# Block products of the delta-rule inverse with B and K together as stationary, in a two-layer RWKV-7 / RG-LRU / mLSTM kernel

## The chip, the cores and the metric

One core of one Trainium2 chip runs the program. The metric is the device time of one execution in microseconds, the median of several runs. TensorE (PE) does matmuls, VectorE (DVE) and ScalarE (ACT) the elementwise work, GpSimd (POOL) little, and SyncE (SP) issues the transfers.

## The reference

The input x is 256 tokens of 2048 features, in float32. Layer 0 (an RG-LRU head group beside an mLSTM head group) is not touched by the change. Layer 1 is RWKV-7 time mixing with 64 heads of 64 features:

```python
u = h @ w_in                                  # columns r, k, v, z, 4096 each
rkv = rkv + (shift_right(rkv) - rkv) * mu_rkv
...                                           # decay w, gate a, kk normalised per head
def step(S, inp):
    r_t, w_t, k_t, v_t, kk_t, a_t = inp
    sa = jnp.einsum('bhvk,bhk->bhv', S, -kk_t)
    S = (S * w_t[:, :, None, :] + sa[..., None] * (kk_t * a_t)[:, :, None, :]
         + v_t[..., None] * k_t[:, :, None, :])
    return S, jnp.einsum('bhvk,bhk->bhv', S, r_t)
...
y = head_norm(y, ...) + bonus                 # bonus = sum(r * k * r_k) * v, per head
return (y * jax.nn.silu(z)) @ w_out
```

The kernel does the scan in four chunks of 64 tokens. In a chunk each token has four rows of 64 features: A (from kk and the decay), R (from r), B (from kk and a) and K (from k). The products of B and K with A and R, masked to earlier tokens, give the matrices of the chunk. The one of B with A has to be inverted (as one minus a strictly triangular matrix).

## The kernel before

Layer 1 works through eight groups g of four feature tiles (128 features, two heads each). Per group there are four in_proj's, in the order k, r, z, v. Each is 192 matmuls into a `gb` bank, from a moving operand of 256 tokens, in pieces of weights split in a high and a low part (`whi`, cast by ACT, and `wlo`, subtracted by DVE, from `raw`). There are three buffers of each, so that wlo of a piece waits until PE is through with the piece three before. After the last group comes out_proj, whose moving operands are split the same way (`yh`, `yl`).

Everything else is written as generators that a class `Weave` (line 58) runs between the matmuls of the stream: four lanes, each generator in a lane after the one before, and each `yield x` says how many microseconds, by the plan, to let pass before its next piece. Lane 0 has `blocks` (927) and `inverse` (986), lane 1 `scores` (951), `values` (1048), `recur` (1089) and `final`, lane 2 `norm`, and lane 3 `decay` and `keys`. The main loop also drains some of them at fixed places: the scores after the z projection, the values of the group before after k. The order in which pieces come out of this is the program's order: PE runs strictly in it (`InOrder`, 102), and so do DVE and ACT as queues. A wait of one instruction therefore holds all that stands behind it on its engine.

The steps of a group that the change touches, in the order of their data:

- `keys` writes AR columns 0:64 (A), Gn (a norm per head) and BK, with B and K next to each other: for one head's 64 rows, B in its own half of the 128 columns and K in the other half.
- `blocks` multiplies, for tile f, chunk c and head hd, 64 columns of BK (B alone, the stationary operand) with A's 64 columns of AR. There are 32 such products, 64x64 each, in two banks (`mbank`; there are four of them); DVE multiplies them with Gn into Aab.
- `scores` writes R into AR's columns 64:128 (four DVE instructions `AR<-rt,Pe`), then takes for each tile f eight products of the whole BK (128 columns) with the whole AR (A and R), 128x128 each, in two banks, and four transposes of BK into a third (L120, then ACT's copy to BKt). DVE masks the banks into At, with `rmask`, in two instructions of 128x512 per tile.
- `inverse` transposes Aab (Ab), solves by 31 pairs of DVE instructions `tf`, `Tb`, waits for recur of the group before, transposes the result into TT and ZT, and finishes it with two sets of small products on PE (`mb<-ZT,Aab`, then with TT).
- `values` makes the bonus: bi, bh and bl from R and K, UV by products with `centre`, the sums by `bonesr`, and vt times them.
- `recur` runs the four chunks with At, BKt, UV and TT.

At, BKt, TT and Rc have one buffer each. L117 and L120 are the lines of the helper through which all matmuls and transposes pass, and L133 that of the elementwise instructions; so the trace tells them apart by their tiles. `f2` counts pairs of tiles.

Of the kernel before, what the change touches and what calls it, by code (L numbers as in the profile page):

```python
# [11 lines left out]
ADD, SUB, MUL, MAX, MIN = ALU.add, ALU.subtract, ALU.mult, ALU.max, ALU.min  # L12

P = 128
# [130 lines left out]
def two_layers(ctx, tc, x, gpost, cst, selc, v0, v1, w_in0, w_out0, w_in1, w_out1, lruw, qkvw,  # L145
               wif, gbias, lora1, lora2, out):
    nc = tc.nc
    act, dve, pool, pe = nc.scalar, nc.vector, nc.gpsimd, nc.tensor
    PS = bass.MemoryType.PSUM
    wv_ = Weave(tc, 4)  # L150
    pe = wv_.pe = InOrder(tc, pe)
    dve, act = Behind(tc, dve), Behind(tc, act)
# [13 lines left out]
    def mbank():  # L166
        return pm.tile([P, 512], F32, name="mb", tag="mb")

    cs = base.tile([P, NC1], F32, name="cs")
    ident = cs[:, C_ID:C_ID + 128]  # L170
# [249 lines left out]
    with ExitStack() as l0:  # L420
# [180 lines left out]
        gt = c0.tile([8, 7, T], F32, name="gt", tag="wg")  # L601
# [119 lines left out]
        for c in range(4):  # L721
# [6 lines left out]
            for f in range(4):  # L728
                i = 4 * c + f
# [44 lines left out]
    with ExitStack() as l1:  # L774
        c1 = l1.enter_context(tc.tile_pool(name="c1", bufs=1))
        g1 = l1.enter_context(tc.tile_pool(name="g1", bufs=1))
        rmask = cs[:, C_RM:C_RM + 128]
# [9 lines left out]
        def gt(name, tag, shape=(4, T), dt=F32, bufs=1):  # L787
            return g1.tile([P, *shape], dt, name=name, tag=tag, bufs=bufs)
# [98 lines left out]
        def keys(g, st):  # L887
# [36 lines left out]
                    yield 0.6  # L924
            st.update(Gn=Gn, AR=AR, BK=BK)

        def blocks(g, st):

            yield from until(st["keys"])
            AR, BK, Gn = st["AR"], st["BK"], st["Gn"]  # L930
            yield 3.5
            Aab = g1.tile([P, 4, 2, 4, 64], F32, name="Aab", tag="c8")
            bs = [mbank(), mbank()]
            for f2 in range(2):
                for f in range(2):
                    for c in range(4):
                        for hd in range(2):
                            hr = slice(64 * hd, 64 * hd + 64)
                            n = (f * 4 + c) * 64
                            pe.matmul(bs[f2][hr, n:n + 64], lhsT=BK[hr, 2 * f2 + f, c, 64 * hd:64 * hd + 64], rhs=AR[hr, 2 * f2 + f, c, 0:64],  # L940
                                      start=(n == 0), stop=True, skip_group_check=True)
            yield 0.5
            for f2 in range(2):
                for hd in range(2):
                    hr = slice(64 * hd, 64 * hd + 64)
                    dve.tensor_tensor(Aab[0:64, 2 * f2:2 * f2 + 2, hd, :, :], bs[f2][hr].rearrange("p (f c i) -> p f c i", f=2, c=4),
                                      Gn[hr, 2 * f2:2 * f2 + 2, :].unsqueeze(3).broadcast_to([64, 2, 4, 64]), MUL)
                    yield 0.9
            st["Aab"] = Aab

        def scores(g, st):
            rt, AR, BK, Pe = st["r"], st["AR"], st["BK"], st["Pe"]
            yield 0.36
            for f in range(4):
                dve.tensor_tensor(AR[:, f, :, 64:128], c4(rt[:, f, :]), Pe[:, 4 * f:4 * f + 4, 1:65], MUL)
                yield 0.5
            yield 2
            Rc = gt("Rc", "Rc", (4, 4, 64))
            act.copy(Rc, AR[:, :, :, 64:128])

            At = gt("At", "At", (4, 2, 4, 128))
            BKt = gt("BKt", "BKt", (4, 4, 128))
            rm4 = rmask.unsqueeze(1).broadcast_to([P, 4, 128])
            for f in range(4):
                ab = [mbank(), mbank()]
                for c in range(4):
                    for hd in range(2):
                        hr = slice(64 * hd, 64 * hd + 64)
                        pe.matmul(ab[hd][:, 128 * c:128 * c + 128], lhsT=BK[hr, f, c, :], rhs=AR[hr, f, c, :],
                                  start=(c == 0), stop=True, skip_group_check=True)  # L970
                b = mbank()
                for c in range(4):
                    pe.transpose(out=b[:, c * P:(c + 1) * P], in_=BK[:, f, c, :], identity=ident)
                yield 0.42
                for hd in range(2):
                    v = ab[hd].rearrange("p (c j) -> p c j", c=4)
                    dve.tensor_tensor(At[:, f, hd, :, :], v, rm4, MUL)
                    yield 1.12
                act.copy(BKt[:, f, :, :], b.rearrange("p (c j) -> p c j", c=4))
            for hd in range(2):  # L980
                hr = slice(64 * hd, 64 * hd + 64)
                act.copy(At[hr, :, hd, :, 0:64], AR[hr, :, :, 0:64])
                yield 0.3
            st.update(At=At, BKt=BKt, Rc=Rc)

        def inverse(g, st):
            Aab = st["Aab"]
# [101 lines left out]
        def recur(g, st):  # L1089
            yield from until(st["inv"])  # L1090
            At, BKt, UV, Rc, Gn, PC, TTv = (st[n] for n in ("At", "BKt", "UV", "Rc", "Gn", "PC", "T"))
# [5 lines left out]
            for c in range(4):  # L1097
                wb = mbank()
                for f in range(4):
                    for hd in range(2):  # L1100
                        hr = slice(64 * hd, 64 * hd + 64)
                        kr = slice(0, P) if c else slice(64 * (1 - hd), 64 * (1 - hd) + 64)
                        pe.matmul(wb[hr, f * 64:(f + 1) * 64], lhsT=At[kr, f, hd, c, 0:64], rhs=UV[kr, c, f, hd, :],
                                  start=(f == 0), stop=True, skip_group_check=True)
# [51 lines left out]
                    yield 0.25  # L1156
                if c == 1:
                    nm = wv_.add(norm(0, Yb, Yn, Yn[:, 1]), 2)
            yT = gt("yT", "Rc", (2, 4, P))
            yield from until(nm)  # L1160
            yield from norm(1, Yb, Yn, yT[:, 1].rearrange("p f (h v) -> p f h v", h=2))
# [186 lines left out]
```

## Time and profile before

| | |
|---|---|
| median of 3 runs | 1887.37 us (1884.68 to 1888.13) |
| the profiled execution | 1884.82 us, span 1883.0 us |
| granted TensorE clock, mean | 0.996 of full |
| PE busy | 1856.2 us, 99% |
| PE's weight loads (PEld) busy | 1723.5 us, 92% |
| DVE busy | 1400.9 us, 74% |
| ACT busy | 1052.2 us, 56% |
| DMA, mean | 161 GB/s |

A fp32 matmul of the program is two instructions in the trace. A row of a timeline gives the start, how long, the engine, the line, what is written from what (out<-in), for PE the rows and columns of the weights and then those of the output, how many instructions follow each other, and in brackets the idle time before the row and who ended it. Ends of PE's instructions are modelled, and its rows overlap; start to start is the safer measure.

### The profile page before, as it was taken

The page shows a single profiled execution, that of the slowest core. Times are in us where ns is not written, and L with a number is a line of the kernel's source. Part 1 is how long each engine was busy: PE and PEld are TensorE (multiplying, and loading weights), DVE is VectorE, ACT ScalarE, POOL GpSimd, SP SyncE. Part 2 cuts the span into 40 slices and gives each one's busy share as a digit, 9 for nine tenths or more (in the row PEclk, how much of TensorE's full clock was granted, in tenths as well). Part 3 has the DMA queues.
Part 4 walks back from the last instruction along what each step waited for, and adds up shares of the span by engine and source line. Part 5 has one row for each costly group of instructions (what it writes and reads, how often), then busy time and mean ns, then how long its engine had stood idle before and what let it go on. Part 6 is the DMA issues. An engine that isn't in the chain of part 4 may idle for free.

```text
span 1883.0 us, 39445 instructions
## 1 busy us (share of the span) xinstructions
PE 1856.2 (99%) x16410; PEld 1723.5 (92%) x16411; DVE 1400.9 (74%) x2279; ACT 1052.2 (56%) x1626; POOL 63.4 (3%) x94
## 2 busy tenths in 40 slices
PE   9999999999999999999999999999999999999998
PEld 8999999999888898999999999999999999987886
DVE  6777777767455668888689789698797896895554
ACT  5446566645444455565565656656656656565442
POOL 0000000000000100000010000000100100000000
PEclk9999999999999999999999999999999999999999
DMA  7543554446566353433433334344344343355654
GB/s 254 189 156 135 180 179 168 158 169 227 194 208 210 138 170 133 147 122 124 147 132 136 136 132 158 124 144 149 119 152 141 131 146 128 130 193 202 214 204 151
DMA packets 95314, 302.66 MB, mean 161 GB/s; under 512 B 11160, under 2 KB 20120, under 8 KB 95136
## 3 DMA queue, kind: packets, MB, share of 16 engines
q1 hardware_dynamic: 95136, 300.16, 46.5%
q8 instruction: 128, 2.10, 0.5%
q14 instruction: 50, 0.41, 0.1%
HBM read 292.25 MB, written 7.86 MB: 159 GB/s over the span
## 4 chain that ended last, share of the span: by engine, by line
PE 92%; DVE 5%; issue 1%; ACT 1%; DMA 1%; POOL 0%; SPq 0%; DVEq 0%; POOLq 0%; ACTq 0%
PE gb L117 75%; PE mb L117 15%; DVE wlo L133 2%; PE mb L120 2%; DVE Tb L133 0%; DVE tf L133 0%; DMA raw<-in_w_in_dram 0%; DVE yT L133 0%; DVE rt L133 0%; ACT whi L133 0%; DMA xq<-in_x_dram 0%; DVE hl L133 0%; POOL vr L1186 0%; DVE AR L133 0%; DVE Ab L133 0%
## 5 line engine op out<-in xcount | busy, mean ns | idle before, releaser
L133 DVE TENSOR_TENSOR wlo<-raw,whi 128x1024 fp32r<-128x1024 f32 (+1 forms) x517 | 627.2, 1214 | 316.7 <-ACT whi L133 278.6
L133 ACT CAST whi<-raw 128x1024 fp32r<-128x1024 f32 (+1 forms) x517 | 538.5, 1044 | 519.5 <-PE gb L117 454.6
L117 PE MATMUL gb<-hh,whi 128*128 128x256 f32 x3120 | 791.6, 290 | 0.6 <-ACT whi L133 0.6
L117 PE MATMUL gb<-hl,whi 128*128 128x256 f32 x3120 | 771.9, 283 | 0.5 <-DVE hl L133 0.5
L117 PEld LDWEIGHTS gb<-hh,whi 128*128 128x128 f32 x3120 | 597.9, 192 | 8.8 <-ACT whi L133 0.8
L117 PEld LDWEIGHTS gb<-hl,whi 128*128 128x128 f32 x3120 | 598.7, 192 | 2.0 <-DVE hl L133 1.1
L117 PE MATMUL gb<-hh,wlo 128*128 128x256 f32 x3120 | 454.5, 286 | 0.0
L117 PEld LDWEIGHTS gb<-hh,wlo 128*128 128x128 f32 x3120 | 405.2, 191 | 3.8
L117 PE MATMUL gb<-whi,yl 128*128 128x512 f32 x500 | 137.2, 392 | 2.0 <-DVE yl L133 2.0
L117 PE MATMUL gb<-whi,yh 128*128 128x512 f32 x500 | 136.2, 391 | 0.0
L117 PE MATMUL gb<-wlo,yh 128*128 128x512 f32 x500 | 135.9, 391 | 0.0
L117 PEld LDWEIGHTS gb<-whi,yl 128*128 128x128 f32 x500 | 93.0, 188 | 22.2 <-DVE yl L133 2.9
L117 PEld LDWEIGHTS gb<-wlo,yh 128*128 128x128 f32 x500 | 93.4, 188 | 19.7
L117 PEld LDWEIGHTS gb<-whi,yh 128*128 128x128 f32 x500 | 93.1, 188 | 19.4
L133 DVE TENSOR_TENSOR Tb<-Tb,tf 64x31 f32<-64x31 f32 (+15 forms) x248 | 82.6, 333 | 6.2
L133 DVE TENSOR_TENSOR tf<-Ab,Tb 64x31 f32<-64x31 f32 (+15 forms) x248 | 81.9, 330 | 4.5
L117 PE MATMUL mb<-AR,BK 64*128 64x128 f32 (+1 forms) x1024 | 60.8, 258 | 11.6 <-DVE AR L133 6.0
L117 PEld LDWEIGHTS mb<-AR,BK 64*128 64x128 f32 (+1 forms) x1024 | 52.3, 165 | 18.5 <-PE gb L117 7.0
L133 DVE TENSOR_TENSOR UV<-mb,Gn 64x256 f32<-64x256 f32 x64 | 27.0, 422 | 34.8 <-PE mb L117 33.6
L117 PEld LDWEIGHTS mb<-UV,At 128*64 128x64 f32 (+1 forms) x1024 | 35.0, 137 | 10.3 <-issue 2.5
L117 PE MATMUL mb<-UV,At 128*64 128x64 f32 (+1 forms) x1024 | 43.8, 228 | 0.0
L133 ACT ACTIVATE zz<-kP,dv 128x256 f32<-128x256 f32 x64 | 32.3, 505 | 20.5 <-DVE BK L133 10.7
(264 smaller groups left out, 1773.1 us busy)
## 6 DMA issues: line engine op xcount, KB each, us to landing
raw<-in_w_in_dram SPq DMA_DIRECT2D x384, 512.0 KB, 3.3
raw<-in_w_out_dram SPq DMA_DIRECT2D x128, 512.0 KB, 4.3
wr<-in_wif_dram SPq DMA_DIRECT2D x48, 80.0 KB, 2.4
y1d<-zt SPq DMA_DIRECT2D x7, 512.0 KB, 3.4
yraw<-y1d SPq DMA_DIRECT2D x7, 512.0 KB, 3.7
xq<-in_x_dram SPq DMA_DIRECT2D x8, 256.0 KB, 5.6
lw<-in_lruw_dram SPq DMA_DIRECT2D x4, 512.0 KB, 4.6
xr<-in_x_dram SPq DMA_DIRECT2D x8, 256.0 KB, 5.7
```

Source lines behind the costliest of these rows:

```text
L117: return self._chain(self.eng.matmul(*a, **k))
L120: return self._chain(self.eng.transpose(**k))
L133: r = op(*a, **k)
```

## The change

Inverse's products in `blocks` take the 128 columns of BK as the stationary operand instead of B's 64, with the same moving columns of A. So a product gives B's rows (for Aab) and K's rows (At's columns of A) at once, in two banks per pair of tiles, one for each head. `blocks` now also masks K's rows into At (four instructions of 64x512) and makes four transposes of BK in each of its halves: `turned` does those of one tile and ACT's copy to BKt (tiles 0 and 1 in `blocks`, 2 and 3 in `scores`). Since At and BKt have one buffer each, `blocks` starts only when `recur` of the group before has set "used". `scores` is left with the moving columns 64:128 (R) and does two tiles at a time; it waits until the blocks have At, and its pause ahead of the products is 6.2 where it was 2.

```diff
@@ -924,29 +924,46 @@
                     yield 0.6
             st.update(Gn=Gn, AR=AR, BK=BK)
 
+        def turned(BKt, BK, f):
+            b = mbank()
+            for c in range(4):
+                pe.transpose(out=b[:, c * P:(c + 1) * P], in_=BK[:, f, c, :], identity=ident)
+            act.copy(BKt[:, f, :, :], b.rearrange("p (c j) -> p c j", c=4))
+
         def blocks(g, st):
 
             yield from until(st["keys"])
             AR, BK, Gn = st["AR"], st["BK"], st["Gn"]
             yield 3.5
+            while g and "used" not in sts[g - 1]:
+                yield 0.44
             Aab = g1.tile([P, 4, 2, 4, 64], F32, name="Aab", tag="c8")
-            bs = [mbank(), mbank()]
+
+            At = gt("At", "At", (4, 2, 4, 128))
+            BKt = gt("BKt", "BKt", (4, 4, 128))
             for f2 in range(2):
+                fs = slice(2 * f2, 2 * f2 + 2)
+                bs = [mbank(), mbank()]
                 for f in range(2):
                     for c in range(4):
                         for hd in range(2):
                             hr = slice(64 * hd, 64 * hd + 64)
                             n = (f * 4 + c) * 64
-                            pe.matmul(bs[f2][hr, n:n + 64], lhsT=BK[hr, 2 * f2 + f, c, 64 * hd:64 * hd + 64], rhs=AR[hr, 2 * f2 + f, c, 0:64],
+                            pe.matmul(bs[hd][:, n:n + 64], lhsT=BK[hr, 2 * f2 + f, c, :], rhs=AR[hr, 2 * f2 + f, c, 0:64],
                                       start=(n == 0), stop=True, skip_group_check=True)
-            yield 0.5
-            for f2 in range(2):
+                turned(BKt, BK, f2)
+                yield 0.5
                 for hd in range(2):
                     hr = slice(64 * hd, 64 * hd + 64)
-                    dve.tensor_tensor(Aab[0:64, 2 * f2:2 * f2 + 2, hd, :, :], bs[f2][hr].rearrange("p (f c i) -> p f c i", f=2, c=4),
-                                      Gn[hr, 2 * f2:2 * f2 + 2, :].unsqueeze(3).broadcast_to([64, 2, 4, 64]), MUL)
+                    dve.tensor_tensor(Aab[0:64, fs, hd, :, :], bs[hd][hr].rearrange("p (f c i) -> p f c i", f=2, c=4),
+                                      Gn[hr, fs, :].unsqueeze(3).broadcast_to([64, 2, 4, 64]), MUL)
                     yield 0.9
-            st["Aab"] = Aab
+                for hd in range(2):
+                    kr = slice(64 * (1 - hd), 64 * (1 - hd) + 64)
+                    dve.tensor_tensor(At[kr, fs, hd, :, 0:64], bs[hd][kr].rearrange("p (f c i) -> p f c i", f=2, c=4),
+                                      rmask[kr, 0:64].unsqueeze(1).unsqueeze(1).broadcast_to([64, 2, 4, 64]), MUL)
+                    yield 0.9
+            st.update(Aab=Aab, At=At, BKt=BKt)
 
         def scores(g, st):
             rt, AR, BK, Pe = st["r"], st["AR"], st["BK"], st["Pe"]
@@ -954,34 +971,32 @@
             for f in range(4):
                 dve.tensor_tensor(AR[:, f, :, 64:128], c4(rt[:, f, :]), Pe[:, 4 * f:4 * f + 4, 1:65], MUL)
                 yield 0.5
-            yield 2
+            while "At" not in st:
+                yield 0.44
+            yield 6.2
             Rc = gt("Rc", "Rc", (4, 4, 64))
             act.copy(Rc, AR[:, :, :, 64:128])
-
-            At = gt("At", "At", (4, 2, 4, 128))
-            BKt = gt("BKt", "BKt", (4, 4, 128))
-            rm4 = rmask.unsqueeze(1).broadcast_to([P, 4, 128])
-            for f in range(4):
+            At, BKt = st["At"], st["BKt"]
+            for f2 in range(2):
                 ab = [mbank(), mbank()]
-                for c in range(4):
-                    for hd in range(2):
-                        hr = slice(64 * hd, 64 * hd + 64)
-                        pe.matmul(ab[hd][:, 128 * c:128 * c + 128], lhsT=BK[hr, f, c, :], rhs=AR[hr, f, c, :],
-                                  start=(c == 0), stop=True, skip_group_check=True)
-                b = mbank()
-                for c in range(4):
-                    pe.transpose(out=b[:, c * P:(c + 1) * P], in_=BK[:, f, c, :], identity=ident)
+                for f in range(2):
+                    for c in range(4):
+                        for hd in range(2):
+                            hr = slice(64 * hd, 64 * hd + 64)
+                            n = (f * 4 + c) * 64
+                            pe.matmul(ab[hd][:, n:n + 64], lhsT=BK[hr, 2 * f2 + f, c, :], rhs=AR[hr, 2 * f2 + f, c, 64:128],
+                                      start=(n == 0), stop=True, skip_group_check=True)
+                turned(BKt, BK, 2 + f2)
                 yield 0.42
                 for hd in range(2):
-                    v = ab[hd].rearrange("p (c j) -> p c j", c=4)
-                    dve.tensor_tensor(At[:, f, hd, :, :], v, rm4, MUL)
+                    dve.tensor_tensor(At[:, 2 * f2:2 * f2 + 2, hd, :, 64:128], ab[hd].rearrange("p (f c i) -> p f c i", f=2, c=4),
+                                      rmask[:, 64:128].unsqueeze(1).unsqueeze(1).broadcast_to([P, 2, 4, 64]), MUL)
                     yield 1.12
-                act.copy(BKt[:, f, :, :], b.rearrange("p (c j) -> p c j", c=4))
             for hd in range(2):
                 hr = slice(64 * hd, 64 * hd + 64)
                 act.copy(At[hr, :, hd, :, 0:64], AR[hr, :, :, 0:64])
                 yield 0.3
-            st.update(At=At, BKt=BKt, Rc=Rc)
+            st.update(Rc=Rc)
 
         def inverse(g, st):
             Aab = st["Aab"]
@@ -1156,6 +1171,7 @@
                     yield 0.25
                 if c == 1:
                     nm = wv_.add(norm(0, Yb, Yn, Yn[:, 1]), 2)
+            st["used"] = True
             yT = gt("yT", "Rc", (2, 4, P))
             yield from until(nm)
             yield from norm(1, Yb, Yn, yT[:, 1].rearrange("p f (h v) -> p f h v", h=2))
```

Where the pieces then stand follows from the weave. Three places are shown, in the program's order (a name is out<-in, then the shape of the output and how often the row repeats).

TensorE in the first group, at the first block products. Before, all 32 in a row and then the first scores:

```order
L117 MATMUL gb<-hh,whi 128x256
L117 MATMUL gb<-hl,whi 128x256
L117 MATMUL mb<-AR,BK 64x64 x32
L117 MATMUL gb<-hh,whi 128x256
L117 MATMUL gb<-hl,whi 128x256
L117 MATMUL gb<-hh,whi 128x256
L117 MATMUL gb<-hl,whi 128x256
L117 MATMUL mb<-AR,BK 128x128 x8
L120 MATMUL mb<-cs,BK 128x128 x4
L117 MATMUL gb<-hh,wlo 128x256 x8
```

Now 16 of them, with four transposes (`mb<-cs,BK`), and the stream goes on:

```order
L117 MATMUL mb<-AR,BK 128x64 x16
L120 MATMUL mb<-cs,BK 128x128 x4
L117 MATMUL gb<-hh,whi 128x256
L117 MATMUL gb<-hl,whi 128x256
L117 MATMUL gb<-hh,whi 128x256
L117 MATMUL gb<-hl,whi 128x256
L117 MATMUL gb<-hh,wlo 128x256 x8
```

The other 16 stand 40 stream matmuls behind these, and the scores, which stood four behind, 136.

TensorE at the blocks of a later group. Before, they stood in the middle of the last chunk of recur (`mb<-UV,At`, `mb<-Sn,Rc`):

```order
L117 MATMUL mb<-UV,At 64x64 x8
L117 MATMUL gb<-hh,whi 128x256
L117 MATMUL gb<-hl,whi 128x256
L117 MATMUL gb<-hh,whi 128x256
L117 MATMUL gb<-hl,whi 128x256
L117 MATMUL mb<-Sn,Rc 64x64 x8
L117 MATMUL gb<-hh,whi 128x256
L117 MATMUL gb<-hl,whi 128x256
L117 MATMUL gb<-hh,whi 128x256
L117 MATMUL gb<-hl,whi 128x256
L117 MATMUL mb<-AR,BK 64x64 x32
```

Now the same neighbours, with half the blocks and transposes:

```order
L117 MATMUL mb<-Sn,Rc 64x64 x8
L117 MATMUL gb<-hh,whi 128x256
L117 MATMUL gb<-hl,whi 128x256
L117 MATMUL gb<-hh,whi 128x256
L117 MATMUL gb<-hl,whi 128x256
L117 MATMUL mb<-AR,BK 128x64 x16
L120 MATMUL mb<-cs,BK 128x128 x4
```

Both follow recur's last products closely; but in the stream of in_proj the blocks and recur with them now stand 92 matmuls later (the second half of the blocks 128), and the first scores 116.

VectorE at the end of the inverse of a later group (the transposes TT and ZT). Before, the values (bi, vt, bl) follow them:

```order
L133 TENSOR_TENSOR Tb<-Tb,tf 64x31
L133 TENSOR_TENSOR wlo<-raw,whi 128x1024
L133 STREAM_TRANSPOSE TT<-Tb 32x32x32 x2
L133 TENSOR_TENSOR wlo<-raw,whi 128x1024
L133 STREAM_TRANSPOSE ZT<-Tb 32x32x32
L133 TENSOR_TENSOR wlo<-raw,whi 128x1024
L133 TENSOR_TENSOR bi<-Rc,BK 64x1024 x2
```

Now they stand ahead of them, bi, vt and bl among the pairs tf, Tb, and vt by mb between TT and ZT:

```order
L133 SCALAR_TENSOR_TENSOR vt<-gb,vec_81,vt 128x255 x2
L133 TENSOR_TENSOR tf<-Ab,Tb 64x135
L133 SCALAR_TENSOR_TENSOR bl<-bi,vec_81,bh 128x256
L133 TENSOR_TENSOR wlo<-raw,whi 128x1024
L133 TENSOR_TENSOR Tb<-Tb,tf 64x5x27
...
L133 STREAM_TRANSPOSE TT<-Tb 32x32x32
L133 TENSOR_TENSOR wlo<-raw,whi 128x1024
L133 STREAM_TRANSPOSE TT<-Tb 32x32x32
L133 TENSOR_TENSOR vt<-vt,mb 128x512 x2
L133 STREAM_TRANSPOSE ZT<-Tb 32x32x32
L133 TENSOR_TENSOR wlo<-raw,whi 128x1024 x4
```

In the first group the values stood ahead of TT and ZT before, too. On TensorE the products with `centre` (of the values) stood 28 stream matmuls behind ZT's product, and now stand 80 ahead of it. In the last group, ZT's product stood 16 matmuls of out_proj after its start, and now 70.

## Rows read from the trace of the kernel before

**Rows 1.** Page, the chain that ended last, by engine.

```profile
PE 92%; DVE 5%; issue 1%; ACT 1%; DMA 1%; POOL 0%; SPq 0%; DVEq 0%; POOLq 0%; ACTq 0%
```

**Rows 2.** PE's waits from 680 us on: us, times, longest.

```profile
PE mb L117 <- DVE AR L133: 6.0, 6, 1.0
PE mb L117 <- DVE BK L133: 2.9, 4, 1.4
PE mb L117 <- DVE At L133: 2.6, 2, 2.2
PE gb L117 <- DVE yl L133: 2.0, 2, 1.5
PE mb L117 <- ACT ZT L133: 0.3, 1, 0.3
```

**Rows 3.** PE's timeline, steady group, blocks and second scores.

```profile
1351.16 2.30 PE L117 MATMUL mb<-AR,BK 64*64 64x64 f32 x64
...
1375.08 0.28 PE L117 MATMUL gb<-hh,whi 128*128 128x256 f32 x1
1375.20 0.28 PE L117 MATMUL gb<-hl,whi 128*128 128x256 f32 x1
1375.41 1.16 PE L117 MATMUL mb<-AR,BK 64*128 64x128 f32 x16
...
1376.91 1.21 PE L117 MATMUL gb<-hh,wlo 128*128 128x256 f32 x8
```

**Rows 4.** PE's groups by shape: busy us, mean ns | idle.

```profile
L117 PE MATMUL mb<-AR,BK 64*128 64x128 f32 x512 | 41.0, 291 | 8.6 <-DVE AR L133 6.0 <-DVE At L133 2.6
...
L117 PE MATMUL mb<-centre,vt 128*128 128x128 f32 x128 | 16.8, 279 | 0.0
```

**Rows 5.** Timeline of PE, products with two moving columns.

```profile
706.11 1.84 PE L117 MATMUL mb<-cs,sq 128*128 128x2 f32 x16
```

**Rows 6.** Timeline of PE at the first group's blocks.

```profile
712.30 1.34 PE L117 MATMUL mb<-AR,BK 64*64 64x64 f32 x32
...
723.02 1.19 PE L117 MATMUL gb<-hh,wlo 128*128 128x256 f32 x8
```

**Rows 7.** Windows: us; PE, PEld, DVE, ACT, POOL; PEclk, DMA, GB/s.

```profile
718.00:719.10 1.10, 1.04 (x15) 0.93 (x15) 0.00 (x1) 0.00 (x0) 0.00 (x0) 0.50 0.00 0
877.70:879.90 2.20, 2.20 (x12) 2.20 (x12) 2.20 (x5) 0.86 (x2) 0.00 (x0) 0.50 0.46 158
1352.50:1423.80 71.30, 70.29 (x614) 68.70 (x611) 68.55 (x122) 37.83 (x54) 1.77 (x2) 1.00 0.42 145
1685.60:1689.00 3.40, 1.89 (x15) 1.78 (x15) 2.10 (x3) 2.14 (x4) 0.00 (x0) 1.00 0.68 241
```

**Rows 8.** Timeline of PE at group 1's second scores.

```profile
873.39 0.48 PE L117 MATMUL mb<-AR,BK 64*128 64x128 f32 x2
876.12 1.64 PE L117 MATMUL mb<-AR,BK 64*128 64x128 f32 x14 [2.24 <-DVE At L133]
...
878.46 0.56 PE L117 MATMUL gb<-hh,whi 128*128 128x256 f32 x1
```

**Rows 9.** DVE's groups by shape: busy us, mean ns | idle.

```profile
L133 DVE TENSOR_TENSOR bi<-Rc,BK 64x1024 f32<-64x1024 f32 x16 | 19.4, 1214 | 0.2
...
L133 DVE SCALAR_TENSOR_TENSOR rt<-gb,vec,rt 128x255 f32<-128x255 f32 x32 | 14.4, 473 | 0.3
...
L133 DVE TENSOR_TENSOR vt<-vt,mb 128x512 f32<-128x512 f32 x16 | 10.2, 679 | 1.6 <-PE mb L117 1.6
...
L133 DVE STREAM_TRANSPOSE TT<-Tb 32x1024 f32<-32x1024 f32 x16 | 32.4, 2025 | 0.3
```

**Rows 10.** Timeline at a steady group's th and ZT.

```profile
1407.26 0.69 DVE L133 TENSOR_SCALAR th<-th 128x1024 f32<-128x1024 f32 x1 [1.09 <-ACT th L133]
...
1423.83 0.62 ACT L133 COPY ZT<-ZT 32x512 f32<-32x512 f32 x1 [1.70 <-DVE ZT L133]
...
1426.31 1.20 PE L117 MATMUL mb<-ZT,Aab 32*32 32x32 f32 x64
```

## The prediction

> **What bounds the kernel now.** I read the chain of work that ended last first: TensorE (PE) carries 92% of the span [rows 1], so a microsecond counts only where PE's stream gains or loses it. Next, the waits of PE in layer 1 (the stretch from 680 us on, where all edited lines run): about 14 us in 1,200 [rows 2]. Three kinds of them belong to the edited code: the first scores of each of six groups wait 1.0 us for VectorE's (DVE's) last columns of AR; the blocks of the first group wait 2.9 us in four pieces for BK; group 1 waits up to 2.2 us for At. The rest is PE's own pace. All other work of a group is an excursion out of the in_proj stream ("gb" matmuls, 0.12 us apart by the two stream rows of [rows 3]), so I price an edit by the time from an excursion's first matmul to the next stream matmul.
>
> **The price of one product.** Each matmul of the program is two instructions in the trace (fp32), so the 32 block products are 64 rows: 2.3 us for the old blocks, 1.50 us for the scores of one tile with its four transposes, plus 1.0 us where AR is late [rows 2, 3]. Inside, (busy minus one instruction) over (count minus one) gives the pace: (1.16−0.29)/15 = 58 ns for the old score product, two heads in turn on the two halves of the rows (the 0.29 is one instruction's mean [rows 4]). The page of weight loads shows what may set it: 128 columns of weights with a moving operand of only two columns run at (1.84−0.29)/15 = 103 ns [rows 5], with nothing else to limit them; two row halves in turn give 52. So 58 is nearly what the loads alone take, and the moving side (128 columns) may take as much.
>
> The Trainium skill (TensorE: Matmul & The Clock Gate, section LDWEIGHTS) says that a load takes P/1.2 ns for P columns, whatever the number of rows: 107 ns for 128, and the row of 103 agrees. It speaks against this change, which doubles the weight columns of every block product; by that figure alone and no overlap a product would cost 107 ns.
>
> The new product is 128 weight columns with 64 moving ones. Its bounds are 52 ns (half of 103) and 58 ns (the old score product, which moves more); if the load were not the limit, it would fall to half of 58, 29 ns (a rival). I take 55, as the weights are exactly those of the scores.
>
> **Part by part, a steady group (2 to 7).** Removed: five excursions, 2.3 + 4×1.50 + 1.0 of wait = 9.3 us, and about 0.09 us of entry each (0.21 from the last stream matmul to the first of the excursion instead of 0.12), 9.7 in all. Added: four excursions (two of blocks, two of scores), each of 32 instructions and four transposes: 1.50 − 16×0.058 = 0.57 that stays, plus 32×0.055 = 1.76, so 2.33; four are 9.3, with entries 9.7. The wait for AR goes, since the scores now stand 92 to 128 stream matmuls behind (11 to 15 us); AR is then long there. Net **0.0 us per group**, bounds −0.4 to +0.4 (52 and 58 ns). DVE's edits cost nothing by count: eight masks of 128x512 become four of 64x512 and four of 128x512, four Aab products stay, and ScalarE (ACT) copies and transposes are as many as before.
>
> **Group 0.** From the start of the blocks at 712.30 to the stream behind the first scores at 723.02 are 10.7 us, with the waits for BK and a granted clock of 0.50 at their end [rows 6, 7]; four stream matmuls in between are 0.5, three more scores 1.50 each. That is 14.7 us. After: BK of the first two tiles is there when the first half comes; the second half comes some 40 stream matmuls later (4.8 us), and its last tile's BK lands about 1.2 us too late (0 to 2.4: DVE now does Aab and At of the first half ahead of it). 4×2.33 + 1.2 = 10.5: **−4.2 us**.
>
> **Group 1.** The At wait: 873.39 to 878.46 is 5.07 us where 1.50 is normal, and the clock stays at 0.50 for the two microseconds behind it [rows 7, 8], some 0.6 us more. 4.2 us of excess; its cause is that group 1's scores waited for free banks and masks in a row, where the new code needs two visits instead of four. Against it I set 0.6 for the two visits standing only 12 stream matmuls apart: **−3.6 us**.
>
> **What moves.** Blocks now wait until recur of the group before is through ("used": At has one buffer). So blocks, inverse and recur run 92 to 108 stream matmuls (11 to 13 us) later. DVE is in order, so this puts the bonus products of `values` (two bi, four bl, four vt, the two vt by mb) ahead of the transposes TT and ZT that end the inverse; they stood behind them. Sum: 2×1.21 + 8×0.47 + 2×0.68 = 7.5 us [rows 9] (bl and vt are instructions like rt's, of the same tile), of which some 7.0 counts since such instructions overlap at their ends; the four rt leave the stretch (4×0.47, 1.7 so counted). So +5.3 us of DVE between blocks and ZT, and 1.0 more in which it waits for the blocks' second half. Against it: PE's way from blocks to ZT's product is longer by 16 stream matmuls (1.9 us) and by the centre products, which now stand ahead of it (16×0.131 = 2.1, [rows 4]): 4.0. And there is slack: DVE is busy 68.55 of 71.30 us in that stretch [rows 7], of which 1.1 us is a true idle before th, and ZT's copy ended at 1424.45 while PE came to it at 1426.31, 1.9 us [rows 10]. 5.3 + 1.0 − 4.0 − 1.1 − 1.9 = −0.7: it just fits. But this is a difference of sums of 70 us; counted only as far as th (which must come before the values) DVE is 2.4 us short, and PE would wait some 2.1 us for ZT. I take **+0.7 us** for each of groups 1 to 6 (0 to 2.1), +4.2. Group 0 had this order before, and waited 0.3 [rows 2]. Queued behind ZT on DVE are four weight pieces' wlo, which PE needs 6 us later at the earliest; behind the waiting PE stands its whole stream.
>
> **The tail.** The last group's inverse runs on into out_proj. TT and ZT now stand behind wlo of a later piece, which waits for PE to free a weight buffer; then two TT of 2.0 [rows 9], a wlo, ZT and its copy (0.6 [rows 10]) follow, some 8 us, and PE, which reaches ZT's product 70 out_proj matmuls in, would wait about 3.4 us (0 to 5.5). The yl waits of before (2.0 [rows 2]) had their place in the same stretch and go: **+1.4 us** (−2 to +3.5).
>
> **Sum.** −4.2 − 3.6 + 0 + 4.2 + 1.4 = −2.2 us on a run of 1884.82 (span 1883.0 and 1.8 around it). The median of the runs is 1887.37, 2.5 above that run; on it I forecast 1885.2. About 0.2% (3.8 us) is what a measurement of this kernel can tell from none.
>
> **The rivals.**
> (a) DVE becomes the bound before ZT. The wait is the 2.1 us of the th count and, as group 1's 2.24 us wait did, drops the clock: there 5.07 − 1.50 − 2.24 = 1.3 and 0.6 behind it, 1.9. [...] Six groups, (2.1 + 1.9 − 0.7)×6 = +20 with the clock lost everywhere, +8 with the clock kept; −2.2 + 14 taken between them: 1899. For it: DVE is at 96% there; against it: the fit above.
> (b) The moving side sets the pace, 29 ns: each excursion loses 32×0.026 = 0.83 us, 32 of them 26.6: 1858. For it: the old score product moves 128 columns, so that its 58 could be the moving side's; against it: 103 ns for a bare load.
> (c) The start gains nothing: group 0's BK wait only moves (with the clock), group 1's At wait becomes one of the second bank. −2.2 + 7.8 = +5.6: 1893. For it: the DVE work of these two groups is what it was; against it: BK of the first half is ready.
> (d) Neither ZT nor the tail waits: −2.2 − 5.6 = −7.8, 1880. For it: the fit of −0.7.
>
> **How the numbers follow.** Forecast 0.47 (0.21 of it faster by over 0.2%, 0.25 within, 0.01 slower; own range 1877 to 1891), (a) 0.20 (0.17 slower, 0.03 within), (b) 0.08 faster, (c) 0.10 (0.06 slower, 0.04 within), (d) 0.15 (0.12 faster, 0.03 within). Faster 0.41, within 0.35, slower 0.24. The range leaves out (b) and the upper half of (a): 1875 to 1899.
>
> **What would show it.** The new products' rows (64*128 weights, 64x64) at 52 to 58 ns and each excursion near 2.3 us; no wait for AR, BK under 1.5 us in all, no At wait over 1 us and no stretch at half clock near 712 to 724 and 870 to 882; waits of PE for ZT in groups 1 to 6, each under 1.5 us, and one in out_proj. Wrong would be: a new wait elsewhere in recur (UV, Ws), since recur now shares DVE with the next group's keys, or Yn's transposes held for a bank; or products at 30 or 100 ns.

## The result, and the profile after

The changed kernel takes 1899.94 us (median of 5 runs, 1892.74 to 1904.35) where the one before takes 1887.37: a ratio of 1.0067, interval 1.0052 to 1.0082. It is slower by 12.6 us, above the upper end of the range (1899.0) and on the other side of the forecast. The profiled execution is the longest of the five (1904.35 us, span 1902.6). One of the eight runs of the last variant below took 10,048 us; it counts in that variant's median and not in its ratio.

PE's waits in layer 1 (from 680 us on; us in total, times, longest) answer to [rows 2]:

```profile
PE mb L117 <- DVE ZT L133: 6.1, 2, 5.7
PE mb L117 <- ACT sq L133: 5.9, 12, 0.8
PE mb L117 <- DVE UV L133: 3.4, 3, 1.7
PE mb L117 <- DVE BK L133: 1.0, 1, 1.0
...
PE mb L117 <- DVE At L133: 0.7, 1, 0.7
```

AR, and the yl of out_proj, are gone from the list, and BK and At are down from 2.9 and 2.6 to 1.0 and 0.7, as forecast. In their place stand sq (the squares of k, from which `keys` makes Gn), ZT and UV. All waits of that list together are 18.5 us against about 14.

The blocks of a steady group answer to [rows 3], and the groups of the new product and of sq to [rows 4, 5] (busy us, mean ns | idle before):

```profile
1368.90 2.00 PE L117 MATMUL mb<-AR,BK 64*128 64x64 f32 x32
1370.83 0.66 PE L120 MATMUL mb<-cs,BK 128*128 128x128 f32 x4
1371.24 0.36 PE L117 MATMUL gb<-hh,whi 128*128 128x256 f32 x1
```

```profile
L117 PE MATMUL mb<-AR,BK 64*128 64x64 f32 x1024 | 64.8, 275 | 1.6 <-DVE BK L133 1.0 <-DVE At L133 0.7
...
L117 PE MATMUL mb<-cs,sq 128*128 128x2 f32 x128 | 17.2, 252 | 5.9 <-ACT sq L133 5.9
```

One visit of 32 instructions is (2.00−0.28)/31 = 55.5 ns per product, and 2.34 us from its start to the stream. All four of a group cost the same, with the entry 2.43 each, 9.7 us: the forecast's 55 ns, 2.33 and 9.7.

The largest part of what the profiled execution lost is TensorE's clock. "Half clock" is a granted clock of 0.50, the lower of its two levels. Adding up, from 680 us on, the length times (1 − granted clock) gives 8.3 us before and 21.4 after (1.5 and 2.6 of it behind PE's last matmul, where it costs nothing). The same kernel in another execution (below) has 9.5 in this sum and a span of 1890.8: the two executions of one program differ by 11.8 us, about as much as their sums.

To see where time goes, I read the start of each stream matmul in both timelines and took the difference, at places where both kernels have the same work behind them (late in the v projection of each group, then the end). All columns count from the start of layer 1; ahead of it the executions differ by up to 0.6 us. After minus before, us:

| at the end of group | 0 | 1 | 2 | 3 | 4 | 5 | 6 | 7 | span's end |
|---|---|---|---|---|---|---|---|---|---|
| changed | −1.8 | −0.4 | 3.0 | 5.1 | 5.8 | 6.5 | 7.2 | 10.7 | 19.7 |
| changed, again | −4.4 | −6.0 | −4.1 | −3.3 | −2.6 | −1.9 | −1.2 | −0.5 | 8.0 |
| old, held | 0.0 | 2.6 | 10.2 | 18.3 | 18.8 | 19.9 | 19.9 | 21.0 | 20.9 |
| new, undelayed | −2.5 | −1.1 | −0.7 | 0.7 | 4.8 | 8.9 | 10.4 | 13.4 | 13.1 |
| wide weights | −3.2 | −0.7 | 0.7 | 3.2 | 6.8 | 9.3 | 11.7 | 14.2 | 14.0 |
| first group, old places | −2.1 | −3.8 | −2.0 | −2.0 | −2.0 | −2.0 | −2.0 | −2.0 | −2.1 |

The second row has little half clock outside out_proj and shows the mechanism nearly bare: a gain of 6.0 us in the first two groups, +1.9 in group 2, where PE waited 0.7 for ZT, +0.7 in each group from 3 on, and +8.5 in out_proj. The first row adds stretches at half clock to it, in groups 0, 1, 2, 3 and 7; in out_proj both have the same 10.2 us of it, part of them while PE waits.

**The steady group.** AR's wait of 1.0 us went and a wait for sq came. PE's rows at sq, then ACT's and DVE's of the same stretch in the changed kernel:

```profile
1461.90 0.95 PE L117 MATMUL mb<-cs,sq 128*128 128x2 f32 x8
1463.01 0.61 PE L117 MATMUL mb<-cs,sq 128*128 128x2 f32 x4 [0.16 <-ACT sq L133]
1464.44 0.61 PE L117 MATMUL mb<-cs,sq 128*128 128x2 f32 x4 [0.82 <-ACT sq L133]
1464.91 0.36 PE L117 MATMUL gb<-hh,whi 128*128 128x256 f32 x1
```

```profile
1458.15 0.36 ACT L133 COPY Ws<-mb 128x256 f32<-128x256 f32 x1
1458.42 0.87 ACT L133 ACTIVATE kt<-gb,dv 128x256 f32<-128x256 f32 x2
...
1460.34 0.51 ACT L133 ACTIVATE sq<-kt,vec 128x256 f32<-128x256 f32 x1 [0.66 <-DVE kt L133]
1461.14 1.06 ACT L133 CAST whi<-raw 128x1024 fp32r<-128x1024 f32 x1 [0.29 <-PE gb L117]
1462.09 0.47 ACT L133 ACTIVATE kt<-gb,dv 128x256 f32<-128x256 f32 x1
...
1463.88 0.51 ACT L133 ACTIVATE sq<-kt,vec 128x256 f32<-128x256 f32 x1 [0.92 <-DVE kt L133]
```

```profile
1462.23 1.23 DVE L133 TENSOR_TENSOR wlo<-raw,whi 128x1024 fp32r<-128x1024 f32 x1 [0.35 <-ACT whi L133]
1463.37 0.48 DVE L133 SCALAR_TENSOR_TENSOR kt<-gb,vec,kt 128x255 f32<-128x255 f32 x1
```

The last kt stands behind a weight piece's cast on ACT, which waits 0.29 us for PE, and then behind that piece's wlo on DVE. So the last sq starts 1.4 us after the one before it (1462.46, left out above). Before, ACT had this order:

```profile
1457.69 0.84 ACT L133 ACTIVATE kt<-gb,dv 128x256 f32<-128x256 f32 x2
...
1459.48 0.47 ACT L133 ACTIVATE kt<-gb,dv 128x256 f32<-128x256 f32 x1
...
1460.31 1.05 ACT L133 CAST whi<-raw 128x1024 fp32r<-128x1024 f32 x1
1461.27 0.90 ACT L133 ACTIVATE sq<-kt,vec 128x256 f32<-128x256 f32 x2
```

All four kt stood ahead of the cast. What is new between them is Ws, the copy of recur's first chunk, which now runs during the k projection of the next group and not before it. That Ws is what pushed the last kt behind the cast is a reading of the two orders; no run took Ws away alone.

**Out_proj.** PE at ZT's product, and DVE ahead of it, in the changed kernel:

```profile
1712.09 0.28 PE L117 MATMUL mb<-ZT,Aab 32*32 32x32 f32 x2 [5.72 <-DVE ZT L133]
1712.65 1.91 PE L117 MATMUL mb<-ZT,Aab 32*32 32x32 f32 x62 [0.27 <-ACT ZT L133]
1714.49 1.22 PE L117 MATMUL gb<-wlo,yh 128*128 128x512 f32 x2
1715.51 1.91 PE L117 MATMUL gb<-whi,yh 128*128 128x512 f32 x4
```

```profile
1704.88 3.94 DVE L133 STREAM_TRANSPOSE TT<-Tb 32x1024 f32<-32x1024 f32 x2
1708.85 1.22 DVE L133 TENSOR_TENSOR wlo<-raw,whi 128x1024 fp32r<-128x1024 f32 x1
1709.99 1.96 DVE L133 STREAM_TRANSPOSE ZT<-Tb 32x1024 f32<-32x1024 f32 x1
```

DVE is never idle there, and PE stands 5.7 us. From 1685 us, shortly before out_proj starts, to ZT's end DVE is busy 26.25 of 26.90 us. The windows behind the wait (us, busy of PE, PEld, DVE, ACT, POOL, then the granted clock) show half speed:

```profile
1712.00:1715.00 3.00, 2.63 (x65) 2.46 (x66) 2.17 (x2) 1.09 (x2) 0.00 (x0) 0.50 0.50 180
1715.00:1720.00 5.00, 5.00 (x13) 3.85 (x12) 1.23 (x1) 1.45 (x3) 0.00 (x0) 0.51 0.76 247
```

### The profile page after: what moved, and what is told of

Same layout as the page of the kernel before. It is cut to its first block, busy times and chain, and to the rows that moved or that the text cites. A ratio compares the mean times of both kernels' runs of the same rounds, so it can differ in the third digit from the quotient of the medians.

```text
span 1902.6 us, 39456 instructions
## 1 busy us (share of the span) xinstructions
PE 1871.4 (98%) x16411; PEld 1742.4 (92%) x16411; DVE 1401.9 (74%) x2279; ACT 1051.4 (55%) x1626; POOL 63.2 (3%) x94
## 5 line engine op out<-in xcount | busy, mean ns | idle before, releaser
L117 PEld LDWEIGHTS gb<-wlo,yh 128*128 128x128 f32 x500 | 93.9, 189 | 19.9
L117 PEld LDWEIGHTS gb<-whi,yh 128*128 128x128 f32 x500 | 93.8, 189 | 19.7
L117 PEld LDWEIGHTS gb<-whi,yl 128*128 128x128 f32 x500 | 93.7, 189 | 19.7
L117 PE MATMUL mb<-AR,BK 64*128 64x64 f32 x1024 | 64.8, 275 | 1.6 <-DVE BK L133 1.0
L117 PEld LDWEIGHTS mb<-AR,BK 64*128 64x128 f32 x1024 | 60.1, 188 | 6.2 <-DVE BK L133 1.1
L133 ACT COPY BKt<-mb 128x512 f32<-128x512 f32 x32 | 18.8, 586 | 57.8 <-PE mb L120 57.8
```

The lines of the kernel that those rows point to most:

```text
L117: return self._chain(self.eng.matmul(*a, **k))
L133: r = op(*a, **k)
```

## The experiments

Two theories stood against each other. **Place**: the loss comes from pieces that meet the queues of DVE and ACT at other places, since the blocks wait for recur. **Product**: the wide products and halved scores themselves cost. Ratios are to the kernel before, measured beside it.

**Held old kernel** (e2_old_held): old products, with the wait alone.

```diff
             yield 3.5
+            while g and "used" not in sts[g - 1]:
+                yield 0.44
             Aab = g1.tile([P, 4, 2, 4, 64], F32, name="Aab", tag="c8")
```

> The kernel before, with one thing added: its blocks, too, wait until recur of the group before is through. By the program's order this moves the blocks of groups 1 to 4 back by 108, 44, 24 and 4 stream matmuls and nothing from group 5 on or in the tail, since the old chain from blocks to recur's end is shorter than a group. Delay theory: a loss in groups 1 to 3 alone, one or two waits of about 1 us for sq or ZT, 1887 to 1892 (ratio 1.000 to 1.003). Product theory: no change, 1887 (ratio 0.999 to 1.001).

Measured: 1905.04, ratio 1.0105 (1.0090 to 1.0120). The place was right (groups 1 to 3, see the table: 2.6, 7.7 and 8.1 us, then 0.0 to 1.1 a group) and the size several times too small. PE's waits from 680 to 1200 us:

```profile
PE mb L117 <- DVE BK L133: 3.1, 4, 1.5
PE mb L117 <- DVE At L133: 2.8, 2, 2.0
...
PE mb L117 <- ACT UV L133: 2.5, 2, 1.9
PE mb L117 <- ACT Ws L133: 1.8, 1, 1.8
```

There are eleven kinds of wait in that stretch. The sum at half clock, from 680 us to the end, is 20.3 us, where the kernel before had 8.3. So a shift of 24 to 108 stream matmuls in three groups, with no new product at all, cost more than the whole change.

**New form with shorter pauses** (e6_recovering): the changed kernel, its wait included; in blocks `yield 0.5` becomes 0.25 and `yield 0.9` 0.45.

> The changed kernel (with its wait for recur of the group before) and only the pauses in blocks halved. By the program's order the delay of the blocks against the kernel before is then 108, 56, 36 and 16 stream matmuls in groups 1 to 4 and none from group 5 on, as in the held old kernel, and the tail stands where it stood. Place theory: groups 5 to 7 and the tail cost what they cost before or less, groups 1 to 4 lose as in the held old kernel (some 20 us there): 1893 to 1905, with no ZT wait in out_proj and no sq waits after group 4. Product theory: as the changed kernel, 1898 to 1902, and a loss in every group.

Measured: 1909.53, ratio 1.0124 (1.0110 to 1.0138), above the range. The tail behaved as expected: from 1300 us on there is no long wait for ZT and none for sq, and yl is as before. The first rows of that list:

```profile
PE mb L117 <- DVE At L133: 2.2, 3, 0.9
PE gb L117 <- DVE yl L133: 1.9, 2, 1.5
...
```

Ahead of that, there are ten kinds of wait while the shift runs through 108, 56, 36 and 16 matmuls; the sum at half clock is 23.2 us. In these runs a steady shift cost less than one that changes with every group.

**Parked** (e1_parked): no wait for recur; K's rows are kept in AtK until the scores come.

```diff
-            while g and "used" not in sts[g - 1]:
-                yield 0.44
...
+            AtK = t4("AtK", (4, 4, 64))
...
+            for hd in range(2):
+                kr = slice(64 * (1 - hd), 64 * (1 - hd) + 64)
+                act.copy(At[kr, :, hd, :, 0:64], AtK[kr])
```

> The new products stay, but K's masked rows of A are parked in a buffer of their own (AtK) and copied into At by ACT when the scores come, and all transposes of BK stay with the scores; so the blocks need not wait for recur of the group before. By the program's order the blocks of a steady group then stand 4 stream matmuls behind their place in the kernel before (92 in the changed kernel). Delay theory (the time is lost because blocks, inverse and recur run some 90 stream matmuls later, where ACT's sq, the last group's ZT and the clock suffer): PE's waits for sq fall from 5.9 us to under 1 us, the time comes to 1880 to 1889, ratio to before 0.996 to 1.001. Product theory (doubled weight columns and halved moving side cost on TensorE): the products are all there, so 1895 to 1900, ratio over 1.004.

Measured: 1918.53, ratio 1.0172 (1.0159 to 1.0185). The time is above both ranges. Removing the wait doesn't put the pieces back: ZT stood 36 matmuls late, behind the centre products. PE's waits in two steady groups and a little more (1240 to 1540 us):

```profile
PE mb L117 <- DVE At L133: 2.7, 3, 0.9
PE mb L117 <- ACT sq L133: 2.1, 4, 0.7
PE mb L117 <- DVE vt L133: 1.7, 2, 0.8
...
```

**Undelayed** (e5_undelayed): as parked, with the pauses of e6 and GpSimd for the copy, so that all but the scores stand in their old places.

> As the parked variant, but the plan's pauses in blocks are halved (0.25 and 0.45, so that blocks as a whole take what they took in the kernel before) and GpSimd, not ACT, copies the parked rows. By the program's order blocks, ZT, centre, sq, Yn and the whole tail then stand exactly where they stand in the kernel before; only the scores stand 40 stream matmuls later. Place theory (the changed kernel loses because its pieces meet the queues of DVE and ACT at other places, not because of the products): no waits for sq, UV, vt or ZT, AR's six waits of 1.0 us gone, 1876 to 1882, ratio 0.995 to 0.999. Product theory (the new products and masks themselves cost): 1893 to 1900, ratio over 1.004.

Measured: 1900.42, ratio 1.0073 (1.0060 to 1.0085). The time is at the upper end of what the product theory gave, far from the place theory's. There is no wait for sq or vt and none for ZT beyond the 0.3 us of before, as the place theory said, and the tail is flat (13.4 to 13.1 in the table); one wait for UV, of 2.4 us, came ahead of 900 us. But AR's waits did not go, they grew; the first of PE's waits from 900 us on:

```profile
PE mb L117 <- DVE AR L133: 8.5, 12, 1.0
...
```

The scores stand 40 matmuls later, but AR's four instructions stand on DVE behind the four rt, steps of tf and Tb, and a wlo, and come later too. So in a steady group the wide products cost 0.8 (9.7 against 2.3 + 1.7 + 1.6 + 1.7 + 1.7 = 9.0 for the old five excursions without AR's wait), and AR 0.4 more; near the table's 1.4 in groups 3 and 6. The other steady groups add half clock. So the wide products are not free; in the changed kernel it was AR's wait, which went, that paid for them.

**Wide weights** (e8_wide_weights): the kernel before, with all of BK as the stationary operand of blocks and K's rows thrown away. The products come in two visits of 32 instructions, with a pause of 0.25 between them.

```diff
-pe.matmul(bs[f2][hr, n:n + 64], lhsT=BK[hr, 2 * f2 + f, c, 64 * hd:64 * hd + 64], rhs=AR[hr, 2 * f2 + f, c, 0:64],
+pe.matmul(bs[hd][:, n:n + 64], lhsT=BK[hr, 2 * f2 + f, c, :], rhs=AR[hr, 2 * f2 + f, c, 0:64],
...
+                yield 0.25
```

> The kernel before, but its block products take all 128 columns of BK as the stationary operand and throw K's rows away (only Aab is made of them); scores, masks, transposes and the places of all pieces are those of the kernel before. So this is the price of the wide product alone: 64 instructions at 58 ns instead of 33, 1.6 us in each of eight groups, and one more excursion's entry: +11 to +15 us, 1896 to 1900, ratio 1.006 to 1.008, if the rows at 58 ns are right; +0 to +3 us if the products hide behind one another.

Measured: 1899.19, ratio 1.0068 (1.0054 to 1.0082), in the range. The table shows +2.5 in each steady group without half clock and not 1.6, and a gain at the start of 3.2. Of the 2.5, the two visits take 1.7 and AR's wait, 1.4 instead of 1.0, takes 0.4; so this is not the price of the product alone.

```profile
1489.78 2.00 PE L117 MATMUL mb<-AR,BK 64*128 64x64 f32 x32
1491.71 0.39 PE L117 MATMUL gb<-hh,whi 128*128 128x256 f32 x1
```

Nothing hides the wider product: 1.93 us from the start of such a visit to the stream, where half of the old blocks took 1.1. And the scores, whose moving columns the change halves, give almost nothing back: 56 ns per product with 64 moving columns, 58 with 128, with the same loads.

**sq later** (e4_sq_later): `yield 2.4` ahead of the sq products becomes 3.9 from group 2 on.

> The changed kernel, with the pause ahead of the sq products of keys 3.9 instead of 2.4 from group 2 on (12 stream matmuls, 1.4 us later). Delay theory: the 1.0 us waits for sq in six groups (1.3 us of excursion each) and the drops of the clock that some of them bring go, 1900 becomes 1889 to 1894 (ratio to before 1.001 to 1.004). If the waits only move to BK, behind the later sums: 1898 to 1902.

Measured: 1912.97, ratio 1.0153 (1.0138 to 1.0167). The time is above both ranges. The sq waits went, and recur's products right behind waited for UV instead, in all six groups. PE's row, and DVE's ahead of it:

```profile
1469.66 0.30 PE L117 MATMUL mb<-UV,BKt 128*64 128x64 f32 x2 [2.26 <-DVE UV L133]
```

```profile
1467.57 1.23 DVE L133 TENSOR_TENSOR wlo<-raw,whi 128x1024 fp32r<-128x1024 f32 x1 [0.34 <-ACT whi L133]
1468.71 0.48 DVE L133 SCALAR_TENSOR_TENSOR kt<-gb,vec,kt 128x255 f32<-128x255 f32 x1
1469.11 0.41 DVE L133 TENSOR_TENSOR UV<-mb,Gn 64x256 f32<-64x256 f32 x1
```

UV stands behind the same late kt that sq waits for. In the changed kernel PE came to UV's products only after it had waited for sq; with that wait taken away, the other shows, and it is longer.

**Tail later** (e3_tail_later): `yield 3.4` ahead of ZT's product becomes 10 in the last group.

> The changed kernel, with the pause ahead of ZT's product 10 instead of 3.4 in the last group alone, which puts that product 30 out_proj matmuls (8 us) later. Delay theory: the wait of 5.7 us for ZT in out_proj and the 7 us at half clock behind it (3.5 us of work lost) go, 1900 becomes 1891 to 1894 (ratio to before 1.002 to 1.004). Product theory: that wait is one of DVE's load and moves elsewhere, 1898 to 1901.

Measured: 1899.18, ratio 1.0068 (1.0056 to 1.0081): no gain. ZT's wait went, and this came in the same stretch:

```profile
1711.40 1.22 PE L117 MATMUL gb<-whi,yl 128*128 128x512 f32 x2 [6.15 <-DVE yl L133]
```

yl stands behind TT and ZT on DVE. The wait is DVE's, whichever product meets it first, as the second expectation had it.

**Tail without bonus** (e9_tail_no_bonus): in `values` the loops for bi, bh, bl, bones and vt run `if g < NG - 1` only.

> The changed kernel, with the last group's bonus left out (bi, bh, bl, their sums by bonesr and the two vt products; part of the computation is missing, so the output is not the reference's). It takes some 6 us of DVE and 0.8 us of TensorE out of the stretch before the last ZT. DVE-bound tail (in out_proj PE waits because DVE has more to do by then than time): the wait of 5.7 us for ZT in out_proj falls under 1 us, and 7 to 10 us go with the half clock behind it: 1889 to 1893 where the changed kernel had 1900. Order theory (TT stands behind a wlo that waits for PE, whatever DVE has to do): the wait stays over 3.5 us, 1896 to 1900.

Measured: 1895.62, ratio 1.0045 (1.0029 to 1.0062), between the two. There is no wait for ZT, but this does not show that DVE's work alone was what PE waited for. The centre products came forward with the removed steps and waited for vt, with half clock behind; counted from the end of in_proj, PE came to ZT's product 5.0 us later than it did in the changed kernel, and DVE, with some 6 us less to do, ended ZT only 2.1 us earlier. PE's waits from 1640 us on, and the reason for the 2.1 on DVE:

```profile
PE mb L117 <- DVE vt L133: 2.8, 2, 2.2
PE mb L117 <- DVE UV L133: 1.7, 1, 1.7
```

```profile
1688.49 1.23 DVE L133 TENSOR_TENSOR wlo<-raw,whi 128x1024 fp32r<-128x1024 f32 x1 [4.15 <-PE gb L117]
```

A wlo that waits for PE stands ahead of TT, as the order theory has it; but PE itself was late there by its new waits, so this variant does not tell the two theories apart. In the changed kernel DVE was hardly idle in this stretch, so there its load set the end of ZT.

**The same kernel again** (e12_changed_again).

> The changed kernel once more, for its trace alone. If the time at half clock follows from the waits, the same waits (sq 1.0 us in six groups, ZT 5.7 us in out_proj) are followed by it at the same places: 720, 800, 830, 940, 1070, 1590, 1710 us. If a wait of about 1 us only sometimes brings it, the waits agree to 0.1 us and the places differ, and the span differs by 3.4 us of half clock (1.7 us of work) for each.

Measured: 1892.71 in the one run, span 1890.8. The waits agree (sq 5.9 in twelve, UV 1.7) but for ZT, 5.4 instead of 5.7, and one of 0.8 for whi that is missing. Of the seven places at half clock only those near 940 and 1710 are there. So the second reading holds: a wait of about 1 us brought half clock only sometimes.

**First group alone** (e10_first_group, e11_first_group_paced, e13_first_group_old_places): the new blocks and scores in group 0, the old ones behind.

```diff
+            wv_.add((blocks if g else blocks0)(g, st))
+            st["scores"] = wv_.add((scores if g else scores0)(g, st), 1)
```

> The new blocks and scores in the first group alone (its blocks need not wait for anything), the old ones in groups 1 to 7, so that from group 1 on blocks stand within 4 stream matmuls of their old places. In the changed kernel's trace and the two others with the new first group, this group gained 2.4 to 4.4 us (waits for BK 2.9 to 1.0, shorter stretch at half clock). Place theory: that gain alone, 1882 to 1884, ratio 0.998 to 0.999. Product theory: as the kernel before within 1 us, since one group's products cost only 0.8 us.

> As the first-group variant, and group 1's scores are paced at 16, 20 and 12 stream matmuls instead of 24, 24 and 0, since their second and fourth waited for At (0.4 and 2.2 us, with the clock dropping) when two stood in a row. Place theory: 3 us less than the first-group variant, 1878 to 1881, ratio 0.996 to 0.998. If the waits for At only spread over the four: the same time as the first-group variant.

> As the paced first-group variant, but the first group's new blocks and scores have halved pauses (0.25 and 0.45) and a pause of 2 ahead of its scores, so that ZT and recur of the first group stand where they stood in the kernel before (4 stream matmuls earlier than in the paced variant), and on DVE the instructions UV of recur stand ahead of the next group's reciprocal and BK again, as before, and not behind them. Place theory: the two waits of PE for UV near 832 us (1.8 and 1.2 us) go, and the half clock behind them: 1877 to 1881, ratio 0.995 to 0.997. Product theory: nothing changes, 1883 as the paced variant.

Measured: 1886.93, ratio 1.0002 (0.9994 to 1.0011); 1883.16, ratio 0.9987 (0.9979 to 0.9996); 1881.59, ratio 0.9972 (0.9962 to 0.9983). All three stand above their place ranges, the last by 0.6 us. The first gained 4.4 us in group 0 and lost 6.6 in group 1, with 6.8 us in its sum at half clock there. Up to 900 us it waits for:

```profile
PE mb L117 <- DVE UV L133: 3.1, 2, 1.8
PE mb L120 <- DVE At L133: 2.3, 1, 2.3
...
```

Pacing took the At wait (down to 0.6). The last variant put recur 4 stream matmuls earlier, so that UV stands ahead of the next group's reciprocal and BK on DVE, and the UV waits of 3.0 us are gone as expected; those for BK (1.7), At (1.4) and ZT (1.3) grew by 2.5 together.

It beats both kernels, the one before by 3.7 us (1885.24 beside it). Against the paced variant its median is 1.6 us lower, but the two intervals overlap and the profiled executions are 1 us apart the other way (spans 1881.4 and 1880.5); what the four stream matmuls were worth is not shown.

## Why the prediction was wrong

Two steps of the sum failed. The term for out_proj was +1.4, and +8.5 and +9.0 were measured. Half clock had no term outside groups 0 and 1, and some 5 of the 12.6 us go with it. Group 1's gain was too large as well.

- **The price of the product: right.** 56 ns for 55, 2.34 us for 2.33, four visits 9.7 for 9.7. The old five excursions, with AR's wait, are 10.0 and not 9.7, since the last two scores take 1.63 and 1.59 us and not 1.50. Rival (b) is out: with 64 moving columns a product takes 56 ns and not 29. A product of 64 weight columns takes 33 ns ((2.30 − 0.22)/63 by [rows 3]; 0.22 is the shortest one). The Trainium skill's rule on weight loads (TensorE: Matmul & The Clock Gate, section LDWEIGHTS: time by columns, not rows) agrees with e8 in its direction: columns double, rows don't, and the product grows. An estimate by its formula, 107 ns for one load of 128 columns, is near the pace of sq's products (103 ns [rows 5]). The 56 ns of two row halves in turn are half of that, so the rule for one load does not give this pace, and the measurement decides.
- **Group 0: right.** −4.2 forecast; −4.4 in one execution of the changed kernel and −1.8 in the other. The 2.6 between them are a wait of 0.84 for whi (688.9 us), ahead of the change, and half clock near 723 us (1.7). BK waited 1.0 for a forecast 1.2.
- **Group 1: wrong by 2 to 5 us.** −3.6 forecast, −1.6 and +1.3 measured. At's wait fell to 0.7 as forecast, but recur of group 0 waited 1.7 for UV near 830 us, with half clock behind it in one of the two. I had no row for UV: I named recur's sharing of DVE with the next keys as what would make the forecast wrong, and gave it no price.
- **Steady groups: the sum nearly right, the term wrong, so the agreement is luck.** +0.7 forecast, +0.7 measured without half clock. I took it for ZT; there it just fitted, as the difference of −0.7 said (one wait in all, 0.7, at group 1's ZT). In group 5 the excursions of blocks and scores are 0.2 cheaper than before with AR's wait, sq costs 1.3 more, ZT's products 0.35 more, and UV's with BKt and centre's 0.6 less. I followed the pieces that the change moves past DVE, and not recur's copies past ACT (by the reading of ACT's order above).
- **Out_proj: the largest miss.** +1.4 forecast; +8.5 in one execution, +9.0 in the other. The wait for ZT was 5.4 to 5.7 and not 3.4, UV's of 1.7 was new, and the half clock behind the wait for ZT, which only rival (a) priced, belonged to this term. The forecast's reason, TT behind a wlo that waits for PE, is not what the changed kernel shows: DVE was busy nearly all of the 27 us ahead of ZT's end, with yl and wlo of out_proj among its work. The mechanism was (a)'s, in one place instead of six.
- **Half clock.** The sum had no term for it outside groups 0 and 1. It makes nearly all of the 11.8 us between two executions. The median of five, 1899.94, stands 7 us above the execution that had little of it. The mean granted clock of every run is on record: at 0.995 the changed kernel's two runs have spans of 1892.7 and 1891.0, and fifteen runs of the kernel before 1884.0 on average. So at the same clock the change costs 7.9 us, near the 8.0 of the table's second row, and the rest of the 12.6, some 5 us, goes with the clock.

The chance of 0.24 for slower, and (a)'s 0.20, were where the result fell; the upper end cut (a) off at half its price, just below the measured time. That (a)'s 1899 comes within 1 us of the median is luck: its waits for ZT in six groups did not come.

What stays open: no run removed the wait for sq or the one for ZT without another wait in its place, so the parts of the 7.9 us are read from the traces and not tried one by one. And e1 and e6 lose some 9 and 6 us more than their longer waits and half clock add up to; of e1's, some 6 may be the wide products (0.8 a group in e5, eight groups), and the rest was not followed.

## What to carry to other kernels

In a kernel whose main engine is full and whose other engines are in-order queues, a wait that is removed by moving pieces can come back at the pieces they are moved to, as it did here: price the new neighbours on every engine, not the wait alone. Try the delay by itself, with the old work, before pricing new work in new places. The first group's gain was lost as long as group 1's scores met waits for At (e10), and was kept where these were spread (e11) and where the other engines' order was brought back as well (e13). When two times differ by microseconds, compare the mean granted clock of the runs first.

## What had not been expected of the hardware

In groups 2 to 7 the 16 products of sq, with two moving columns each, were followed by half clock without any wait in 6 of 30 cases (five kernels, the granted clock from sq's start to 8 us later at 0.79 or less), and with the waits of 0.16 and 0.82 in 9 of 24 (the changed order of these groups, four executions). AR's waits of 1.0 us, with wide products on either side, were followed by it in none of 18, those of 0.96 and 0.46 (e5) in 3 of 6, and e4's waits of 2.26 and 0.44 in 6 of 6. So the length of a wait alone doesn't tell whether half clock follows; what does was not settled here. Each piece cost 1.7 us or twice that.
